# A hybrid decoder layer on one core: the sums of left operands and the late block sums of the second part move from GpSimd to VectorE

## The chip, the core and the metric

The kernel runs on one core of a Trainium2 chip. A core has five engines with instruction queues of their own: TensorE (PE in the profile, with its weight loads as PEld), VectorE (DVE), ScalarE (ACT), GpSimd (POOL) and SyncE (SP, which here only issues DMAs). Each queue is worked off in order; engines wait for each other through semaphores. The metric is the device time of one execution in microseconds, smaller is better.

## What is computed

One layer with two branches, on 2048 tokens and 16 meta tokens of width 1024, in float32:

```python
u = rmsnorm(hres, norm_w)
proj = jnp.einsum('bld,dn->bln', u, w_in)          # one projection for all
...                                                # branch 1: Mamba-2 SSD; branch 2: gated linear attention
branches = jnp.stack([y_ssd, y_gla], axis=2)
branch_proj = jnp.einsum('blnc,ncd->blnd', branches, w_branch)
gates = jax.nn.sigmoid(merge_g.reshape(b, l, N_BRANCH, D_MODEL))
merged = jnp.sum(gates * branch_proj, axis=2)
return hres + jnp.einsum('bld,de->ble', merged, w_out)   # then a final rmsnorm
```

The first part of the kernel computes the projections and the two branches; the second part computes the gates, the branch projections, the merge and the output projection, which are plain matrix products.

## The kernel before

**First part** (to about 1487 us). Four blocks of 512 tokens are projected and scanned. It isn't touched. Beside its work, GpSimd forms for later use the block sums of right operands of most stages (`make_sums` with a `store`; its line L84).

**Second part.** Seven stages follow each other: gate0, br00, br10 for the first half of the tokens, gate1, br01, br11 for the second half, and out. Each is a product of matrices that is done with seven instead of eight block products (the Strassen-Winograd scheme): a stage has 8 pairs (gate and out) or 4 (br), two pairs are worked on together, and each pair needs seven products p in the order 1, 2, 6, 7, 5, 3, 4. There are 280 products. A product is four accumulated steps of three matmuls each (L193 to L195): both operands are split into a high and a low half in float32r, and high-high, high-low and low-high are added up.

What a product needs:

- **Right operands** `br` (128 x 512, raw) are loaded by SP at L1011, 28 for each stage, through 5 buffers. ACT writes the high half of `b` (L1016), DVE subtracts it for the low half (L1017). When DVE has done so, the buffer of `br` is free and SP can load the next.
- **Left operands** `ar` are loaded by SP at L1023, four blocks a11, a12, a21, a22 for each pair, through 8 buffers, which is two pairs. From them come four sums: s1 = a21 + a22 (L1031), s2 = s1 - a11 (L1032), a21 = a11 - a21 in place (L1033) and s4 = a12 - s2 (L1034). GpSimd makes them. For each product ACT then writes the high half of `a` (L1040) and DVE the low half (L1041), five products ahead, into 7 buffers. An `ar` buffer is free when the last of these readers is done.
- **Results.** Products 1, 6 and 5 are copied from PSUM to `sn` by ACT (L1057). DVE adds `sn` to a PSUM bank (L1068: psc or psb); in the br stages it multiplies by the gate (L1094), in the out stage it adds the residual (L1117) and, after a norm (L1121 to L1132), GpSimd's queue stores the rows. PSUM bank `psa` can only take the next product when `sn` has been copied, and `psb` can only take product 4 when L1068 has read product 5.
- **Late block sums.** The right operands' sums of br01 and br11 can't be formed in the first part, since the tokens come last. `make_sums` is called for them with `store` None: SP loads four blocks (L80), GpSimd makes four differences of 128 x 256 (L84), and GpSimd's queue stores them two products later. There are 16 such units, eight in gate0 and eight in gate1, five products apart.

GpSimd's queue also issues all stores of the second part (L991, and L994 with an addition in memory).

The order on PE and on SP is written out: a table `todo` gives each load and preparation a place relative to the products (a right operand is loaded 3.2 places ahead of its preparation, a left one 7.5 ahead of its first product). On DVE, ACT and GpSimd a scheduler puts the instructions in order, by a timing of its own, when the kernel is built.

Of the kernel before, what the change touches and what calls it, by code (L numbers as in the profile page):

```python
# [12 lines left out]
ALU = mybir.AluOpType  # L13
# [27 lines left out]
def trunk_kernel(ctx: ExitStack, tc: tile.TileContext, xm, xmt, w_feat, w_tok, w_zm, w_br, w_o,  # L41
                 cf32, cmsk, pvec, fnw, hvec, gw2, out):
    nc = tc.nc
# [5 lines left out]
    def mk(pool, shape, dt, tag, **kw):  # L49
        cnt[0] += 1  # L50
        return pool.tile(shape, dt, tag=tag, name=f"{tag}_{cnt[0]}", **kw)
# [24 lines left out]
    def make_sums(pool, tag, nb, braw, sums, j, c, store):  # L76
        cs = slice(c * HB, (c + 1) * HB)
        pair = [mk(pool, [P, 512], F32, tag, bufs=nb).rearrange("p (i c) -> p i c", i=2) for _ in range(2)]
        for r, (k, t) in zip((t[:, i] for t in pair for i in range(2)), ((0, 1), (0, 0), (1, 1), (1, 0))):
            nc.sync.dma_start(r, braw(4 * k + j, t)[:, cs])  # L80
        yield
        (b12, b11), (b22, b21) = [(t[:, 0], t[:, 1]) for t in pair]
        for o, x, y in ((b11, b12, b11), (b12, b22, b12), (b22, b22, b11), (b21, b21, b22)):
            nc.gpsimd.tensor_tensor(o, x, y, op=ALU.subtract)  # L84
        if store is None:
            for dst, src in zip(sums, pair):
                late_store(dst[j][:, :, cs], src, 2)
            return
        yield
        yield  # L90
        for dst, src in zip(sums, pair):
            store.dma_start(dst[j][:, :, cs], src)
# [3 lines left out]
    def late_store(dst, src, lag=1):  # L96
        stores.setdefault(step_no[0] + lag, []).append((dst, src))
# [295 lines left out]
    def new_block(b, u):  # L393
        o = Block()
        o.b, o.u = b, u
        o.m0 = META if b == 0 else 0
        o.tt = o.m0 + BLK
        o.segs_all = [(0, o.tt // 2), (o.tt // 2, o.tt // 2)] if b == 0 else [(0, BLK)]
        o.segs_real = [(o.m0, BLK)]
        o.starts = [o.m0 + c * P for c in range(NCH)]  # L400
        o.chunks = ([(0, META)] if o.m0 else []) + [(a, P) for a in o.starts]
        o.ci0 = 1 if o.m0 else 0
        o.nck = len(o.chunks)
        for nm in ("tkd", "tkc", "ntc", "wde", "ecu", "dec"):
            setattr(o, nm, mk(bpool, [P, 5, NH], F32, nm, bufs=1))
        o.cumd = mk(dpool, [NH, BLK], F32, "cumd")
        o.g_all = mk(bpool, [P, GH, META + BLK], F32, "g_all")
        o.both = None
        if o.m0:
            o.both = mk(early, [P, KT, 2 * META], F32R, "both", bufs=1)  # L410
            for i in range(2):
                nc.gpsimd.tensor_copy(o.both[:, :, i * META:(i + 1) * META], u[i][:, :, :META].bitcast(F32))
        o.alr = mk(bpool, [P, 5, 48], F32, "alr")
        o.mov = lambda kt, a, n: tuple(t[:, kt, a:a + n] for t in u)
        return o
# [515 lines left out]
    def beside_unit(key):  # L931
        for j in range(4):
            for c in range(2):
                yield from make_sums(early, "wr", NWR, *sums[key], j, c, nc.sync)

    with tc.manual_schedule(engines={mybir.EngineType.PE, mybir.EngineType.SP}):
        for b in range(nblk):
            o = new_block(b, next_u[b])
# [45 lines left out]
    store = late_store  # L984
# [11 lines left out]
    class Stage:  # L996
# [23 lines left out]
        def load_a(self, n):  # L1020
            def raw(i, j):
                t = mk(rpl, [P, 4, P], F32, "ar")
                nc.sync.dma_start(t, self.araw(n, i, j))  # L1023
                return t

            if n not in self.a:
                self.a[n] = raw(0, 0), raw(0, 1), raw(1, 0)
                return
            (a11, a12, a21), a22 = self.a[n], raw(1, 1)
            s1, s2, s4 = [mk(spl2, [P, 4, P], F32, "as") for _ in range(3)]  # L1030
            nc.gpsimd.tensor_tensor(s1, a21, a22, op=ALU.add)  # L1031
            nc.gpsimd.tensor_tensor(s2, s1, a11, op=ALU.subtract)  # L1032
            nc.gpsimd.tensor_tensor(a21, a11, a21, op=ALU.subtract)  # L1033
            nc.gpsimd.tensor_tensor(s4, a12, s2, op=ALU.subtract)  # L1034
            self.a[n] = {1: a11, 2: a12, 3: s4, 4: a22, 5: s1, 6: s2, 7: a21}

        def prep_a(self, n, p):
# [140 lines left out]
    begun_at = [begins[3 * s] for s in range(nsb)]  # L1178
    spots = [g + 9 + 5 * k for g in begun_at for k in range(8)]
    late_sums = [make_sums(opl, "io", 8, *sums[key], j, c, None) for key in late for j in range(4) for c in range(2)]  # L1180
    for pos, gen in zip(spots, late_sums):
        for k in range(2):
# [104 lines left out]
```

## Time and profile before

| | |
|---|---|
| median of 3 runs | 2296.2 us (2296.17 to 2300.63) |
| profiled execution | span 2298.3 us from the first to the last instruction |
| second part: first product to last | 1487.4 to 2283 us |
| L1031 to L1034 on GpSimd | 160 of 128 x 512, means 1476 to 1653 ns |
| L84 on GpSimd in the second part | 64 of 128 x 256, means 867 and 913 ns |

The execution's own time is not listed apart from its span. In the rows of the profile, `a<-ar` says that tile `a` is written from tile `ar` (buffer numbers left out). A row of the timeline gives start, duration, engine, line and operation, and in brackets the idle time ahead of it with what ended it; x2 means that two instructions were put together. A row of groups gives busy time in us, mean in ns, then the engine's idle time ahead of it. A row of windows gives the stretch, its length, the busy time of PE, PEld, DVE, ACT and POOL with the number of instructions, the granted clock of TensorE, the busy share of the DMA engines and GB/s.

### The profile page before, as it was taken

The page shows a single profiled execution, that of the slowest core. Times are in us where ns is not written, and L with a number is a line of the kernel's source. Part 1 is how long each engine was busy: PE and PEld are TensorE (multiplying, and loading weights), DVE is VectorE, ACT ScalarE, POOL GpSimd, SP SyncE. Part 2 cuts the span into 40 slices and gives each one's busy share as a digit, 9 for nine tenths or more (in the row PEclk, how much of TensorE's full clock was granted, in tenths as well). Part 3 has the DMA queues.
Part 4 walks back from the last instruction along what each step waited for, and adds up shares of the span by engine and source line. Part 5 has one row for each costly group of instructions (what it writes and reads, how often), then busy time and mean ns, then how long its engine had stood idle before and what let it go on. Part 6 is the DMA issues. An engine that isn't in the chain of part 4 may idle for free.

```text
span 2298.3 us, 36496 instructions
## 1 busy us (share of the span) xinstructions
PE 2223.2 (97%) x12599; PEld 1938.7 (84%) x12599; DVE 1646.5 (72%) x3108; ACT 1119.4 (49%) x2508; POOL 789.6 (34%) x869
## 2 busy tenths in 40 slices
PE   6899999999999999999999999989999999999998
PEld 6899888888889889888988898868787788788786
DVE  5787767687765687775678656687778855788775
ACT  5565554463444454444445434554644545454443
POOL 3344533122221122212212100158535476535452
PEclk9999999999999999999999999999999999999999
DMA  7767866667886676886677654466767866679653
GB/s 254 232 221 245 296 211 208 211 193 246 267 264 208 205 225 208 272 278 206 203 215 230 215 184 149 149 221 205 264 233 223 249 216 213 233 251 252 182 185 110
DMA packets 281866, 507.51 MB, mean 221 GB/s; under 512 B 27104, under 2 KB 134880, under 8 KB 281680
## 3 DMA queue, kind: packets, MB, share of 16 engines
q1 hardware_dynamic: 217232, 413.76, 55.7%
q0 software_dynamic: 17568, 50.87, 7.3%
q10 hardware_dynamic: 46880, 40.54, 5.4%
q8 instruction: 99, 1.62, 0.3%
q14 instruction: 87, 0.71, 0.1%
HBM read 357.87 MB, written 147.19 MB: 220 GB/s over the span
## 4 chain that ended last, share of the span: by engine, by line
PE 73%; DVE 9%; DMA 9%; issue 4%; ACT 3%; POOL 2%; SPq 1%; ACTq 0%; POOLq 0%; DVEq 0%
PE pj L193 13%; PE pj L195 13%; PE pj L194 13%; PE psa L193 4%; PE psa L195 4%; PE psa L194 4%; DMA br<-br_t 2%; PE psb L195 2%; PE psb L193 2%; PE psb L194 2%; DVE b L1017 2%; PE pc L619 2%; PE pc L789 2%; PE pc L889 1%; PE pc L620 1%
## 5 line engine op out<-in xcount | busy, mean ns | idle before, releaser
L193 PE MATMUL pj<-u,whl 128*128 128x512 f32 (+1 forms) x1184 | 445.5, 376 | 9.4 <-ACT acc L529 4.5
L195 PE MATMUL pj<-u,whl 128*128 128x512 f32 (+1 forms) x1184 | 429.5, 363 | 0.0
L194 PE MATMUL pj<-u,whl 128*128 128x512 f32 (+1 forms) x1184 | 428.9, 362 | 0.0
L193 PE MATMUL pj<-whl,u 128*128 128x256 f32 (+1 forms) x992 | 288.8, 291 | 2.8 <-ACT u L261 2.2
L195 PE MATMUL pj<-whl,u 128*128 128x256 f32 (+1 forms) x992 | 282.4, 285 | 0.2 <-DVE u L266 0.2
L194 PE MATMUL pj<-whl,u 128*128 128x256 f32 (+1 forms) x992 | 282.1, 284 | 0.0
L193 PE MATMUL psa<-b,a 128*128 128x512 f32 x640 | 252.3, 394 | 18.1 <-ACT sn L1057 17.9
L193 PEld LDWEIGHTS pj<-u,whl 128*128 128x128 f32 x1184 | 223.6, 189 | 47.2 <-ACT acc L529 5.4
L195 PEld LDWEIGHTS pj<-u,whl 128*128 128x128 f32 x1184 | 223.2, 188 | 35.6
L194 PEld LDWEIGHTS pj<-u,whl 128*128 128x128 f32 x1184 | 223.9, 189 | 33.1
L194 PE MATMUL psa<-b,a 128*128 128x512 f32 x640 | 250.2, 391 | 0.9 <-DVE b L1017 0.9
L195 PE MATMUL psa<-b,a 128*128 128x512 f32 x640 | 250.5, 391 | 0.0
L84 POOL TENSOR_TENSOR wr<-wr 128x256 f32<-128x256 f32 x80 | 64.2, 803 | 428.8 <-DMA wr<-u 163.4
L181 POOL TENSOR_TENSOR whl<-wr,whl 128x512 fp32r<-128x512 f32 (+1 forms) x100 | 138.3, 1389 | 187.2 <-ACT whl L180 154.8
L1041 DVE TENSOR_TENSOR a<-ar,a 128x512 fp32r<-128x512 f32 x160 | 157.3, 993 | 61.9 <-ACT a L1040 61.4
L1017 DVE TENSOR_TENSOR b<-br,b 128x512 fp32r<-128x512 f32 x196 | 159.1, 833 | 49.1 <-ACT b L1016 48.8
L193 PEld LDWEIGHTS pj<-whl,u 128*128 128x128 f32 x992 | 189.8, 191 | 4.5 <-ACT u L261 2.3
L195 PEld LDWEIGHTS pj<-whl,u 128*128 128x128 f32 x992 | 189.8, 191 | 0.8 <-DVE u L266 0.8
L194 PEld LDWEIGHTS pj<-whl,u 128*128 128x128 f32 x992 | 189.9, 191 | 0.4
L1016 ACT ACTIVATE b<-br 128x512 fp32r<-128x512 f32 x196 | 120.1, 628 | 125.2 <-DMA br<-br_t 53.6
L533 DVE SCALAR_TENSOR_TENSOR acc<-cin,hcw,acc 128x512 f32<-128x512 f32 (+1 forms) x192 | 161.3, 840 | 11.4 <-ACT acc L529 9.3
L193 PEld LDWEIGHTS psa<-b,a 128*128 128x128 f32 x640 | 120.9, 189 | 49.3 <-ACT sn L1057 24.7
(297 smaller groups left out, 5064.5 us busy)
## 6 DMA issues: line engine op xcount, KB each, us to landing
whl<-k_s SPq DMA_DIRECT2D x96, 512.0 KB, 4.4
whl<-k_g SPq DMA_DIRECT2D x96, 512.0 KB, 4.2
whl<-k_v SPq DMA_DIRECT2D x48, 512.0 KB, 4.0
whl<-k_z SPq DMA_DIRECT2D x36, 512.0 KB, 4.1
wr<-in_w_feat SPq DMA_DIRECT2D x64, 256.0 KB, 4.4
k_s<-whl SPq DMA_DIRECT2D x32, 512.0 KB, 3.8
cb<-cumd ACTq DMA_DIRECT2D x64, 256.0 KB, 5.8
k_g<-whl SPq DMA_DIRECT2D x32, 512.0 KB, 3.8
```

The source lines that it names most:

```text
L84: nc.gpsimd.tensor_tensor(o, x, y, op=ALU.subtract)
L181: nc.gpsimd.tensor_tensor(hl[:, 1], raw, hl[:, 0].bitcast(F32), op=ALU.subtract)
L193: nc.tensor.matmul(ps, sh, mh, start=first, stop=False, **kw)
L194: nc.tensor.matmul(ps, sh, ml, start=False, stop=False, **kw)
L195: nc.tensor.matmul(ps, sl, mh, start=False, stop=last, **kw)
L533: nc.vector.scalar_tensor_tensor(acc, cin[:, k:k + tt], hcw[:, ti, k:k + 1], acc, op0=ALU.mult, op1=ALU.add)
L619: nc.tensor.matmul(py[:, h * 64:(h + 1) * 64], dm[:, h], xdt[:, h], start=True, stop=True)
L620: nc.tensor.matmul(py[:, 256:512], cf[:, a:a + P], s_ssd[:, g], start=True, stop=True)
L789: nc.tensor.matmul(ps[:, r * P:(r + 1) * P], kq[:, 2 * r * P:(2 * r + 1) * P], kq[:, (2 * r + 1) * P:(2 * r + 2) * P], start=True, stop=True)
L1016: nc.scalar.activation(t[:, 0], raw, AF.Copy)
L1017: nc.vector.tensor_tensor(t[:, 1], raw, t[:, 0].bitcast(F32), op=ALU.subtract)
L1041: nc.vector.tensor_tensor(t[:, 1], src, t[:, 0].bitcast(F32), op=ALU.subtract)
```

## The change

The four sums of left operands are issued on VectorE, in all seven stages, and so are the differences of `make_sums` where `store` is None, which is the late ones. The block sums beside the first part stay on GpSimd, as do all stores.

```diff
-            nc.gpsimd.tensor_tensor(o, x, y, op=ALU.subtract)
+            (nc.vector if store is None else nc.gpsimd).tensor_tensor(o, x, y, op=ALU.subtract)
...
-            nc.gpsimd.tensor_tensor(s1, a21, a22, op=ALU.add)
-            nc.gpsimd.tensor_tensor(s2, s1, a11, op=ALU.subtract)
-            nc.gpsimd.tensor_tensor(a21, a11, a21, op=ALU.subtract)
-            nc.gpsimd.tensor_tensor(s4, a12, s2, op=ALU.subtract)
+            nc.vector.tensor_tensor(s1, a21, a22, op=ALU.add)
+            nc.vector.tensor_tensor(s2, s1, a11, op=ALU.subtract)
+            nc.vector.tensor_tensor(a21, a11, a21, op=ALU.subtract)
+            nc.vector.tensor_tensor(s4, a12, s2, op=ALU.subtract)
```

224 instructions leave GpSimd's queue and join DVE's. The orders of PE and SP stay the same, word for word; on DVE and ACT the scheduler rearranges the second part. Three places follow; a row with + stands there now, one with - stood there before, and the others stand in both.

DVE at the start of the second part, from rstd (the last norm of the first part) to the second `b2`; `b2` are the right operands of product 2, `end_g` belongs to the first part's end:

```order
 L241 TENSOR_SCALAR rstd_2956_17162<-ssq_2944_17087 128x4
+L1031 TENSOR_TENSOR as_2965_17303<-ar_2963_17299,ar_2964_17301 128x512
+L1032 TENSOR_TENSOR as_2966_17304<-as_2965_17303,ar_2961_17295 128x512
+L1033 TENSOR_TENSOR ar_2963_17299<-ar_2961_17295,ar_2963_17299 128x512
 L1041 TENSOR_TENSOR a_2984_17348<-ar_2968_17310,a_2984_17348 128x512
+L1034 TENSOR_TENSOR as_2967_17305<-ar_2962_17297,as_2966_17304 128x512
 L1041 TENSOR_TENSOR a_2989_17363<-ar_2962_17297,a_2989_17363 128x512
+L1031 TENSOR_TENSOR as_2972_17318<-ar_2970_17314,ar_2971_17316 128x512
 L1041 TENSOR_TENSOR a_2994_17374<-ar_2969_17312,a_2994_17374 128x512
+L1032 TENSOR_TENSOR as_2973_17319<-as_2972_17318,ar_2968_17310 128x512
+L1033 TENSOR_TENSOR ar_2970_17314<-ar_2968_17310,ar_2970_17314 128x512
 L1041 TENSOR_TENSOR a_2999_17389<-as_2966_17304,a_2999_17389 128x512
```

Right behind these rows comes the first `b2` (L1017), then `end_g`, the eighth sum, `end_g` again and the second `b2`; ahead of the third and of the fourth `b2` there are now two L1041 each, which stood behind them before.

DVE at the handover from gate1 to br01; `b6` and `b7` are right operands of br01, the first two `a` are the last ones of gate1 (product 4), `as` are sums for br01:

```order
 L1017 TENSOR_TENSOR b6_3778_21518<-br_3750_21413,b6_3778_21518 128x512
+L1041 TENSOR_TENSOR a_3758_21442<-ar_3696_21106,a_3758_21442 128x512
 L1017 TENSOR_TENSOR b6_3781_21538<-br_3756_21427,b6_3781_21538 128x512
-L1041 TENSOR_TENSOR a_3758_21442<-ar_3696_21106,a_3758_21442 128x512
 L1017 TENSOR_TENSOR b6_3784_21546<-br_3760_21448,b6_3784_21546 128x512
+L1031 TENSOR_TENSOR as_3763_21468<-ar_3754_21422,ar_3762_21466 128x512
 L1041 TENSOR_TENSOR a_3766_21475<-ar_3705_21145,a_3766_21475 128x512
+L1032 TENSOR_TENSOR as_3764_21469<-as_3763_21468,ar_3752_21418 128x512
+L1033 TENSOR_TENSOR ar_3754_21422<-ar_3752_21418,ar_3754_21422 128x512
 L1017 TENSOR_TENSOR b7_3788_21569<-br_3768_21481,b7_3788_21569 128x512
```

and ACT at the same place, where `sn` is the copy of a product:

```order
 L1016 ACTIVATE b6_3778_21518<-br_3750_21413 128x512
-L1016 ACTIVATE b6_3781_21538<-br_3756_21427 128x512
 L1057 ACTIVATE sn_3744_21385<-psa_3724_21266 128x512
 L1040 ACTIVATE a_3758_21442<-ar_3696_21106 128x512
+L1016 ACTIVATE b6_3781_21538<-br_3756_21427 128x512
 L1016 ACTIVATE b6_3784_21546<-br_3760_21448 128x512
```

On both engines the first `a` moved ahead of `b6_3781`, and one sum now stands ahead of the second `a`.

DVE at the handover from br11 to out, with the right operands `b6` and `b7` of out, the last `a` of br11 (a_4070) and sums of out:

```order
 L1017 TENSOR_TENSOR b6_4089_23010<-br_4063_22908,b6_4089_23010 128x512
+L1031 TENSOR_TENSOR as_4066_22928<-ar_4056_22880,ar_4065_22926 128x512
 L1041 TENSOR_TENSOR a_4070_22937<-ar_4006_22615,a_4070_22937 128x512
+L1032 TENSOR_TENSOR as_4067_22929<-as_4066_22928,ar_4054_22876 128x512
+L1033 TENSOR_TENSOR ar_4056_22880<-ar_4054_22876,ar_4056_22880 128x512
+L1034 TENSOR_TENSOR as_4068_22930<-ar_4055_22878,as_4067_22929 128x512
 L1041 TENSOR_TENSOR a_4082_22978<-ar_4054_22876,a_4082_22978 128x512
 L1017 TENSOR_TENSOR b7_4092_23032<-br_4072_22943,b7_4092_23032 128x512
```

One sum came ahead of a_4070, and three ahead of the next `a` and `b7`.

## The prediction

> **What bounds the kernel now.** I read the page first, for the busiest engine.
>
> ```profile
> PE 2223.2 (97%) x12599; PEld 1938.7 (84%) x12599; DVE 1646.5 (72%) x3108; ACT 1119.4 (49%) x2508; POOL 789.6 (34%) x869
> ```
>
> PE is the bound of the whole. The change touches only the second part, so I cut that part into windows and read busy time by engine (the first number behind the stretch is its length).
>
> ```profile
> 1493.00:1513.00 20.00, 12.33 (x51) 9.29 (x49) 18.42 (x21) 11.96 (x24) 10.24 (x10) 0.83 0.41 138
> ...
> 1640.00:1650.00 10.00, 7.75 (x33) 5.77 (x32) 8.02 (x8) 5.58 (x10) 9.92 (x7) 1.00 0.74 250
> 1650.00:1720.00 70.00, 70.00 (x310) 57.98 (x310) 51.00 (x71) 36.40 (x65) 22.93 (x27) 1.00 0.68 237
> ...
> 1798.00:1830.00 32.00, 28.82 (x117) 22.69 (x117) 29.91 (x37) 16.82 (x31) 17.91 (x14) 0.95 0.82 225
> ...
> 1956.00:1966.00 10.00, 4.31 (x15) 3.19 (x14) 7.63 (x7) 3.53 (x6) 8.14 (x6) 0.86 0.68 219
> ...
> 2120.00:2157.00 37.00, 32.56 (x142) 25.97 (x141) 28.77 (x39) 18.11 (x35) 15.33 (x13) 1.00 0.89 235
> ...
> sum 789.00, PE 763.20 PEld 625.76 DVE 590.63 ACT 387.88 POOL 411.50; mean PE 63.60 PEld 52.15 DVE 49.22 ACT 32.32 POOL 34.29
> ```
>
> The sum row covers 1493 to 2282: PE idles 789.0 - 763.2 = 25.8 us. That idle time, and a few us of half clock behind it (the granted clock of 0.83 and 0.86), is all that any change here can win. It lies in knots: 7.7 us at the start (1493), then 2.3, 3.2, 5.7 and 4.4 us where one stage hands over to the next. Between them PE is full (1650:1720: 70/310 = 0.226 us a matmul, so a product of 12 matmuls takes 2.7 us). DVE at 591 of 789 (75%) is next. The table of waits says whom PE waits for.
>
> ```profile
> PE psa L193 <- ACT sn L1057: 17.9, 13, 5.7
> PE psc L194 <- DVE b L1017: 6.7, 2, 4.0
> ```
>
> **What DVE pays for GpSimd's sums.** The groups of instructions, with their means in ns:
>
> ```profile
> L1041 DVE TENSOR_TENSOR a<-ar,a 128x512 fp32r<-128x512 f32 x159 | 156.6, 995 | 61.9 <-ACT a L1040 61.4
> L1017 DVE TENSOR_TENSOR b<-br,b 128x512 fp32r<-128x512 f32 x192 | 156.5, 836 | 48.6 <-ACT b L1016 48.4
> L1041 DVE TENSOR_TENSOR a<-as,a 128x512 fp32r<-128x512 f32 x120 | 125.7, 1048 | 37.7 <-ACT a L1040 36.8
> L1068 DVE TENSOR_TENSOR sn<-sn,psb 128x512 f32<-128x512 f32 x78 | 53.1, 682 | 35.3 <-ACT sn L1057 24.6 <-PE psb L195 10.5
> ...
> L84 POOL TENSOR_TENSOR io<-io 128x256 f32<-128x256 f32 x32 | 28.7, 913 | 0.1
> ...
> L779 DVE TENSOR_TENSOR sq<-sq,act 128x256 f32<-128x256 f32 x14 | 5.9, 422 | 1.0 <-ACT sq L778 0.5 <-PE pt L871 0.2
> ```
>
> L1068 has the same shape, runs in the same stretches, and takes 682 ns; it reads one operand from PSUM. L1041 and L1017 read both from SBUF and average 836 to 1048. The surplus is 159 x 0.313 + 120 x 0.366 + 192 x 0.154 = 123 us. That it comes from GpSimd's sums is seen at single rows of the start:
>
> ```profile
> 1497.64 5.07 DVE L1017 TENSOR_TENSOR b<-br,b 128x512 fp32r<-128x512 f32 x1
> ...
> 1498.44 1.28 POOL L1032 TENSOR_TENSOR as<-as,ar 128x512 f32<-128x512 f32 x1
> ...
> 1500.88 1.27 POOL L1034 TENSOR_TENSOR as<-ar,as 128x512 f32<-128x512 f32 x1
> ...
> 1502.77 0.79 PE L194 MATMUL psc<-b,a 128*128 128x512 f32 x1 [4.03 <-DVE b L1017]
> ...
> 1512.64 2.49 DVE L1017 TENSOR_TENSOR b<-br,b 128x512 fp32r<-128x512 f32 x4
> ```
>
> One L1017 stood 5.07 us while GpSimd ran its sums from 1498.44 to 1502.15, and PE waited 4.03 us for it. With GpSimd silent, four took 2.49 us: (2.49 - 0.69)/3 = 0.60 us apart.
>
> **The load of DVE.** Added: 160 sums L1031 to L1034 at 0.68 us (the L1068 row) = 109 us, and 64 of L84 at 0.42 us (the L779 row) = 27 us, together 136 us. Removed: the 123 us. DVE's load hardly moves, whereas GpSimd gives up nearly all its arithmetic here. The removal is the unknown: at none of it DVE would stand at 727 of 789 us (92%), at all of it near 604. I take all, because of the 682 of L1068. So the time is decided by order, not by load; I follow it through the knots.
>
> **Start: -3 us.** As the order shows, DVE does eleven other operations between rstd (row below) and the first L1017, which itself is the twelfth.
>
> ```profile
> 1489.65 0.17 DVE L241 TENSOR_SCALAR rstd<-ssq 128x4 f32<-128x4 f32 x1 [1.05 <-ACT junk L896]
> ```
>
> 1489.8 + 12 x 0.60 + about 0.4 for sums that wait for the one ahead = 1497.4, as before (1497.7). The second L1017 is four places on, at 1499.9 instead of 1502.7; the third and fourth come behind two L1041 each, at 1501.7 and 1503.5. PE then waits in three short pieces, and ends this product about 2 us earlier. The two L1017 for the next products follow at once and not several us later, which takes 1 us more.
>
> **gate1 to br01, the 5.7 us gap: -3.4 us.** The chain in rows:
>
> ```profile
> 1951.22 0.63 ACT L1016 ACTIVATE b<-br 128x512 fp32r<-128x512 f32 x1 [3.69 <-DMA br<-br_t]
> ...
> 1952.90 1.40 DVE L1041 TENSOR_TENSOR a<-ar,a 128x512 fp32r<-128x512 f32 x1 [0.31 <-ACT a L1040]
> ...
> 1955.91 1.78 DVE L1041 TENSOR_TENSOR a<-ar,a 128x512 fp32r<-128x512 f32 x1
> ...
> 1954.32 3.73 SPq L1023 DMA_DIRECT2D ar<-in_w_br  x2
> 1958.10 0.43 SPq L1011 DMA_DIRECT2D br<-br_t  x1
> ...
> 1961.67 1.30 ACT L1016 ACTIVATE b<-br 128x512 fp32r<-128x512 f32 x2 [6.73 <-DMA br<-br_t]
> ...
> 1963.51 0.80 PE L193 MATMUL psa<-b,a 128*128 128x512 f32 x1 [5.69 <-ACT sn L1057]
> ```
>
> SP stood at two loads of left operands until the two L1041 freed their slots (ends 1954.30 and 1957.69); only then, at 1958.10, came the right operands for which ACT waited ahead of the copy sn that PE needed. After the change ACT and DVE do the first of these L1041 ahead of the b that waits until 1951.2, so it no longer holds SP. The second follows two L1017 and one sum: ACT's b ends at 1951.85, then four steps of 0.60, so it ends near 1954.3, 3.4 us earlier. SP, the loads, ACT and PE move with it.
>
> **Other boundaries: about -0.6 us in sum.** Here the change also hurts:
>
> ```profile
> 2114.47 2.40 DVE L1041 TENSOR_TENSOR a<-ar,a 128x512 fp32r<-128x512 f32 x2
> ...
> 2115.04 1.28 POOL L1031 TENSOR_TENSOR as<-ar,ar 128x512 f32<-128x512 f32 x1 [6.80 <-DMA ar<-m]
> ...
> 2115.18 0.52 SPq L1023 DMA_DIRECT2D ar<-m  x1
> ...
> 2122.43 0.50 PE L193 MATMUL psa<-b,a 128*128 128x512 f32 x1 [1.45 <-ACT sn L1057]
> ...
> 2143.17 0.50 PE L193 MATMUL psa<-b,a 128*128 128x512 f32 x1 [1.41 <-ACT sn L1057]
> ```
>
> The sum, whose operand landed at 2115.0, now stands ahead of the L1041 that releases SP at 2115.18; that L1041 ends near 2116.3, +1.1 us on this gap. The like holds, at 0.6 us each, at three more boundaries (gate0 to br00, br00 to br10, br01 to br11): +2.9. Behind it, each operation that ran beside a sum at 1.7 us now takes 0.60, so the later loads of the same handover leave 1 to 3 us earlier; I count -1 on the gap of 1.41 at 2143, and as much on the later gaps of two more handovers (around 1744 and 1827) = -3, and -0.5 at 1805, where the releasing L1041 was itself slowed. The 64 operations of L84 lie in the gate stages, where PE hardly idles; their loads landed before DVE reaches most of them, so they cost nothing. If that cover were gone, 27 us.
>
> **Sum:** -3 - 3.4 + 2.9 - 3 - 0.5 = **-7 us**. It is made in an execution of 2298.3 us of span (its own time apart from the span isn't listed); the median of the runs is 2296.2, 2.1 below, and what lies around these knots is unchanged, so: 2289.
>
> **A rule weighed.**
>
> ```profile
> 1805.66 0.50 PE L193 MATMUL psa<-b,a 128*128 128x512 f32 x1 [2.54 <-ACT sn L1057]
> ...
> 1806.71 0.63 PE L193 MATMUL psa<-b,a 128*128 128x512 f32 x1
> ...
> 2155.94 0.50 PE L193 MATMUL psa<-b,a 128*128 128x512 f32 x1 [1.58 <-ACT sn L1057]
> ```
>
> Behind 2.54 us of idle time the matmuls lasted 0.63 us, behind 1.58 they didn't slow down. The gap that I shorten to 5.7 - 3.4 = 2.3 us lies between the two, so the sum leaves its slow matmuls (about 8 at 0.2 us more) in. The Trainium skill, "TensorE: Matmul & The Clock Gate", section "Part 1: The HAM clock gate", has the clock halved after an idle window of about 3.4 us; the 2.54 us here disagree, and by that rule the sum would be -8.6.
>
> **Rivals.** (1) *Full clock behind the shortened gap*: -7 - 1.6, **2287**. For it: 1.58 us did no harm. Against: 2.54 did. (2) *The loads pace the handovers, and the gains and delays cancel*: the 5 slots of br and loads of several us stay. If start and gate1 to br01 bring half (-3.2) and the second gaps gain only 1: -3.2 + 2.9 - 1 = -1.3, **2295**. For it: ACT's waits in these rows end with DMAs. (3) *Slower: DVE, in order, now waits where GpSimd waited alone.*
>
> ```profile
> 2223.18 0.69 DVE L1117 SCALAR_TENSOR_TENSOR io<-sn,io 128x512 f32<-128x512 f32 x1
> ...
> 2228.56 1.43 POOL L1031 TENSOR_TENSOR as<-ar,ar 128x512 f32<-128x512 f32 x1 [6.73 <-DMA ar<-m]
> ```
>
> In the new order this sum stands ahead of the L1117 of 2223.18, so DVE stops for some 5.4 us, and behind it L1041s and the L1068 that frees psb. PE needs that bank three products (8 us) after it was filled; DVE catches up at 0.60 us a step with about 3 us to spare, and L1041s are made five products (13 us) ahead. Should the operand land over 3 us later than here, each us more stops PE. At eight such places 1.5 us each: -7 + 12 = +5, **2301**. Against: the spare time. (4) *The change does nothing*, were DVE's surplus not GpSimd's; 2296, counted with (2): the 5.07 row speaks against it.
>
> **How the numbers follow.** Forecast 0.55 (own range 2283 to 2292), (1) 0.08, (2) and (4) 0.22, (3) 0.15. A measurement of this kernel can tell about 0.2%, 4.6 us. Forecast's upper end, 0.05, lies within that, so faster 0.58, same 0.27, slower 0.15. The range runs from 2280 (a little more than twice the forecast gain, still within the idle time) to 2301, which leaves out half of (3) and the case where none of DVE's surplus goes.
>
> **What would show it.** Right: L1041 and L1017 at a mean near 690 ns, DVE near 600 us, the start's idle time at 4 to 5 us, the 5.7 us gap near 2.3, the one at 2122 longer. Wrong: L1041 staying near 1000 ns; new PE gaps within stages, at psb, with DVE idle ahead of L1031; SP waiting longer for L1041.

## The result, and the profile after

| | before | after |
|---|---|---|
| median of the runs | 2296.8 us (6 runs, 2292.74 to 2300.63) | 2285.4 us (6 runs, 2279.01 to 2290.58) |
| ratio after / before | | 0.9941 (95% interval 0.9925 to 0.9958) |
| profiled span | 2298.3 us | 2288.8 us |
| second part, first product to last | 799.4 us | 784.2 us |

The change makes the kernel 11 us faster by the medians and 13.5 by the ratio. Forecast were 7, so the direction and the range held and the gain was larger than worked out. The last row is the sharper measure, and by it the gain is 15 us, twice the forecast: in the profiles below, the second part begins anywhere from 1483.0 to 1493.1 us although the first part's work is the same in all but the last of them, and this scatter of 10 us lies in every single time. The rows of windows over the second part, of the kernel before and then of the change (stretch, length, busy PE, PEld, DVE, ACT, POOL, clock, DMA):

```profile
1487.45:2286.80 799.35, 773.55 (x3371) 633.60 (x3370) 598.11 (x746) 394.28 (x727) 416.29 (x426) 0.99 0.69 218
...
1493.08:2277.28 784.20, 771.69 (x3371) 633.46 (x3370) 577.67 (x970) 394.35 (x727) 130.68 (x203) 0.99 0.70 222
```

TensorE's idle time falls from 799.35 - 773.55 = 25.8 us to 12.5. VectorE does 224 instructions more and is busy 20 us *less*. The groups of the change say why:

```profile
L1017 DVE TENSOR_TENSOR b<-br,b 128x512 fp32r<-128x512 f32 x192 | 127.8, 688 | 30.6 <-ACT b L1016 30.2
L1041 DVE TENSOR_TENSOR a<-ar,a 128x512 fp32r<-128x512 f32 x160 | 109.5, 689 | 70.1 <-ACT a L1040 69.8
L1041 DVE TENSOR_TENSOR a<-as,a 128x512 fp32r<-128x512 f32 x120 | 82.7, 690 | 28.1 <-ACT a L1040 27.3
L1068 DVE TENSOR_TENSOR sn<-sn,psb 128x512 f32<-128x512 f32 x80 | 54.8, 685 | 22.1 <-PE psb L195 12.7 <-ACT sn L1057 9.1
L1031 DVE TENSOR_TENSOR as<-ar,ar 128x512 f32<-128x512 f32 x40 | 27.6, 690 | 29.4 <-DMA ar<-m 19.7 <-DMA ar<-in_w_feat 6.4 <-DMA ar<-in_w_br 3.1
...
L84 DVE TENSOR_TENSOR io<-io,io 128x256 f32<-128x256 f32 x32 | 13.5, 423 | 0.4
```

L1041, 995 and 1048 ns before, and L1017, 836 before, all take what L1068 always took. VectorE now waits 29 us ahead of L1031 for loads that GpSimd used to wait for. TensorE's waits in the second part of the change:

```profile
PE psa L193 <- ACT sn L1057: 8.6, 7, 2.2
PE psc L194 <- DVE b L1017: 3.2, 4, 1.6
```

They were 17.9 and 6.7 us.

To see where the time went I add up, for every matmul of the second part, the time from one start to the next beyond the usual 0.2265 us (so slow matmuls at half clock count too), by place. "again" is a second profile of the same program, taken as e5 below.

| us lost at | before | change | change again | forecast for the change |
|---|---|---|---|---|
| start | 11.8 | 9.8 | 9.3 | -3 |
| gate0 to br00 | 2.8 | 4.0 | 2.3 | +0.6 |
| br00 to br10 | 1.7 | 0 | 0 | +0.6 - 1 |
| br10 to gate1 | 5.6 | 2.6 | 1.7 | -1 - 0.5 |
| gate1 to br01 | 7.5 | 2.4 | 3.9 | -3.4 |
| br01 to br11 | 0.5 | 0 | 2.0 | +0.6 |
| br11 to out | 5.2 | 1.3 | 1.5 | +1.1 - 1 |
| sum | 35.2 | 20.2 | 20.7 | -7 |

The count takes in the first part's last matmuls, which lie among the first products. The sums of two profiles of one program agree within 0.5 us, the single places only within 2. For e5 each place's idle time was expected within 1 us of the first profile's, and the median at 2282 to 2288; br01 to br11 missed it, with 1.76 us of idle time instead of none.

### The profile page after: what moved, and what is told of

It reads as the page before. It is cut to its first block, busy times and chain, and to the rows that moved or that the text cites. A ratio compares the mean times of both kernels' runs of the same rounds, so it can differ in the third digit from the quotient of the medians.

```text
span 2288.8 us, 36364 instructions
## 1 busy us (share of the span) xinstructions
PE 2224.8 (97%) x12599; PEld 1941.6 (85%) x12599; DVE 1624.2 (71%) x3332; ACT 1119.7 (49%) x2508; POOL 507.4 (22%) x645
## 4 chain that ended last, share of the span: by engine, by line
PE 78%; DVE 7%; DMA 6%; issue 3%; ACT 3%; POOL 1%; SPq 1%; ACTq 0%; POOLq 0%; DVEq 0%
PE pj L193 13%; PE pj L195 13%; PE pj L194 13%; PE psa L193 5%; PE psa L195 5%; PE psa L194 5%; PE psb L195 3%; PE psb L194 3%; PE psb L193 3%; PE pc L619 2%; PE pc L789 2%; PE psc L195 1%; PE psc L194 1%; PE psc L193 1%; PE pc L620 1%
## 5 line engine op out<-in xcount | busy, mean ns | idle before, releaser
L1016 ACT ACTIVATE b<-br 128x512 fp32r<-128x512 f32 x196 | 119.7, 627 | 86.7 <-DMA br<-br_t 36.7
L84 POOL TENSOR_TENSOR wr<-wr 128x256 f32<-128x256 f32 x80 | 67.2, 840 | 424.3 <-DMA wr<-u 174.0
L1041 DVE TENSOR_TENSOR a<-ar,a 128x512 fp32r<-128x512 f32 x160 | 109.5, 689 | 70.1 <-ACT a L1040 69.8
L1017 DVE TENSOR_TENSOR b<-br,b 128x512 fp32r<-128x512 f32 x196 | 130.5, 688 | 31.3 <-ACT b L1016 30.9
```

Source lines behind the costliest of these rows:

```text
L84: (nc.vector if store is None else nc.gpsimd).tensor_tensor(o, x, y, op=ALU.subtract)
L1016: nc.scalar.activation(t[:, 0], raw, AF.Copy)
L1017: nc.vector.tensor_tensor(t[:, 1], raw, t[:, 0].bitcast(F32), op=ALU.subtract)
L1041: nc.vector.tensor_tensor(t[:, 1], src, t[:, 0].bitcast(F32), op=ALU.subtract)
```

## Experiments

The theory: GpSimd's sums stretched VectorE's operations on two SBUF operands, and the chains of such steps at the handovers and at the start became longer; without it they are short, and VectorE has the time for the sums. Rivals: the scheduler's new order on VectorE and ScalarE brought the gain (R1); GpSimd's queue is free for the stores sooner (R2); VectorE's load decides, whatever it is made of (R3). Each run stands against the kernel before, whose median was 2296.7 to 2299.1 us in these comparisons.

| | median us | ratio to before (95%) | second part us |
|---|---|---|---|
| e1 left sums only | 2290.1 | 0.9969 (0.9959 to 0.9979) | 789.4 |
| e2 late sums only | 2302.8 | 1.0028 (1.0017 to 1.0038) | 801.1 |
| e3 change + GpSimd additions | 2374.3 | 1.0332 (1.0312 to 1.0352) | 867.1 |
| e4 change + GpSimd memsets | 2286.7 | 0.9957 (0.9941 to 0.9973) | 788.3 |
| e5 change again | 2281.9 | 0.9929 (0.9914 to 0.9944) | 784.6 |
| e6 change, 10 left buffers | 2274.9 | 0.9895 (0.9881 to 0.9910) | 776.2 |
| e7 before, 10 left buffers | 2304.5 | 1.0023 (1.0012 to 1.0034) | 799.7 |
| e8 no sums at the start | 2281.8 | 0.9919 (0.9904 to 0.9934) | 780.6 |
| e9 first pairs only | 2287.7 | 0.9957 (0.9943 to 0.9971) | 789.2 |
| e10 more work on VectorE | 2285.0 | 0.9943 (0.9923 to 0.9964) | 786.1 |
| e11 9 left, 6 right buffers | 2283.9 | 0.9942 (0.9920 to 0.9965) | 781.1 |
| e12 all block sums | 2288.3 | 0.9964 (0.9949 to 0.9978) | 777.2 |

### e3 and e4: is it the stretching?

To the change, behind the sums in `load_a`, for e3 and for e4 (`dead` is a tile of its own, set to zero at the start):

```diff
+            [nc.gpsimd.tensor_tensor(dead, dead, x, op=ALU.add) for x in (a22, dead, dead, dead)]
```

```diff
+            nc.gpsimd.tensor_tensor(dead[:, 0, 0:1], dead[:, 0, 0:1], a22[:, 0, 0:1], op=ALU.add)
+            [nc.gpsimd.memset(dead, 0.0) for _ in range(10)]
```

e3:

> The change, and behind each set of left sums GpSimd does four additions of 128x512 on a tile that nobody uses, the first with a22 as operand, so that they start when the sums started before. It leaves the result as it is; orders of TensorE, SyncE are those of the change, VectorE's and ScalarE's nearly so. Theory (stretching): L1041 and L1017 go back to means of 900 to 1050 ns, VectorE carries the stretch and the sums, some 700 us of the 790, and the time goes back to the one before or past it: 2295 to 2310. Rival 1 (order): within 3 us of the change, 2282 to 2289, though VectorE's means rise. Rival 2 (GpSimd's queue): 2295 or more, and the next kernel as well.

e4:

> The change, and behind each set of left sums GpSimd does a wait on a22 of one column and ten memsets of 128x512 on a tile that nobody uses: its queue is as busy as before, but it reads no SBUF operands. Theory (stretching by operands read from SBUF): L1041 and L1017 stay under 750 ns and the time within 3 us of the change, 2282 to 2289. Rival 1 (order): the same. Rival 2 (GpSimd's queue holds up stores): 2293 or more with VectorE's means near 690 ns. If memsets stretch VectorE too, its means show it, and the time follows them.

Groups of e3 (the second part):

```profile
L1035 POOL TENSOR_TENSOR dead<-dead 128x512 f32<-128x512 f32 x120 | 161.7, 1348 | 8.0
L1041 DVE TENSOR_TENSOR a<-ar,a 128x512 fp32r<-128x512 f32 x160 | 132.8, 840 | 46.4 <-ACT a L1040 46.2
...
L1033 DVE TENSOR_TENSOR ar<-ar,ar 128x512 f32<-128x512 f32 x40 | 55.4, 1385 | 0.0
```

Groups of e4:

```profile
L1035 POOL MEMSET dead<- 128x512 f32 x400 | 215.8, 539 | 20.7
L1041 DVE TENSOR_TENSOR a<-ar,a 128x512 fp32r<-128x512 f32 x160 | 109.3, 688 | 67.9 <-ACT a L1040 67.4
...
L1033 DVE TENSOR_TENSOR ar<-ar,ar 128x512 f32<-128x512 f32 x40 | 27.4, 685 | 0.0
```

160 additions on GpSimd, of which nobody uses the result, cost 92 us against the change (2374.3 against 2281.9; 83 us by the second parts), far more than expected; the stretch falls mostly on the sums, which run beside them (L1033 from 686 to 1385 ns), less on L1041 (840 instead of the 900 to 1050 expected). 400 memsets, which keep GpSimd about as busy, stretch nothing and cost 1 to 5 us. So R2 falls (e4), and R1 falls as the whole cause: e3 has nearly the change's order (on VectorE 962 of the second part's 983 instructions stand in the same succession) and none of its gain. That the order brings a part of the gain isn't excluded by e3; e10 bears on it. GpSimd slows VectorE by reading SBUF, not by being busy. The Trainium skill, "SBUF — State Buffer", section "Who interferes with whom", says just this: a VectorE instruction with two SBUF inputs contends with a GpSimd instruction that reads SBUF, not with one that only writes it. The 688 and the 1385 ns agree.

### e10: is it VectorE's load?

The same four additions on VectorE instead:

```diff
+            [nc.vector.tensor_tensor(dead, dead, x, op=ALU.add) for x in (a22, dead, dead, dead)]
```

> The change, and behind each set of left sums VectorE does four more additions of 128x512 on a tile that nobody uses: 160 instructions, about 97 us at 0.60, without GpSimd. VectorE then has some 680 us to do in 785, as in the kernel before, but nothing is stretched. The scheduler sets its order anew. Theory: within the stages this costs nothing; where the additions stand in the chain of a handover each costs 0.6, so up to 2.4 us at the start and at each of six handovers: 3 to 12 us over the change. If load without stretching costs nothing at all: within 2 us of the change. If load is what made the kernel before slow: back to it, 10 us or more over the change.

The second part of e10, and three rows of its timeline (VectorE, then TensorE):

```profile
1488.64:2274.71 786.07, 769.96 (x3371) 631.60 (x3370) 662.76 (x1131) 393.03 (x727) 129.14 (x203) 1.00 0.70 222
...
2226.85 0.69 DVE L1031 TENSOR_TENSOR as<-ar,ar 128x512 f32<-128x512 f32 x1 [1.22 <-DMA ar<-m]
...
2229.87 0.68 DVE L1068 TENSOR_TENSOR sn<-sn,psb 128x512 f32<-128x512 f32 x1
...
2230.60 0.50 PE L193 MATMUL psb<-b,a 128*128 128x512 f32 x1 [2.84 <-DVE sn L1068]
```

VectorE is busy 663 us of 786, 65 more than in the kernel before, and the time is that of the change within 2 us of second part. R3 falls: load as such is nearly free, a stretched chain is not. The rows show one price: at two places in the out stage a sum, and the additions with it, hold the L1068 behind them until TensorE lacks `psb`. That is the slower rival of the prediction; it needed twice the work to appear, and gaps of 1.43 and 2.84 us came of it.

The near equality is a balance, though. Counted as in the table, e10 loses about 6.8 us at the start (the change 9.8 and 9.3) and 6.7 from br11 to out on (the change 1.3 and 1.5). Its order at the start is another: the second L1017 begins 1.2 us behind the first, and not 2.5 as in the change. So an order can be worth some 3 us at one place, and the additions cost more than the sum shows. On VectorE e10's order is far from the change's (700 of 983 instructions in the same succession) and the gain is about the same, so the gain doesn't hang on the change's own order; what part of it the new order brings at single places stays open.

### e1 and e2: the two halves

e1 is the change with L84 as before, e2 the kernel before with this line of the change:

```diff
-            nc.gpsimd.tensor_tensor(o, x, y, op=ALU.subtract)
+            (nc.vector if store is None else nc.gpsimd).tensor_tensor(o, x, y, op=ALU.subtract)
```

e1:

> Half of the change: the left operands' sums (L1031 to L1034) on VectorE, the late block sums (L84) still on GpSimd. Theory: the gain comes from VectorE's operations no longer being stretched by GpSimd's sums of two SBUF operands, and the left sums are nearly all of those that run beside handovers, so nearly all of the 11.4 us should be there: 8 to 11 us under the kernel before. L1041 and L1017 at means of 700 to 740 ns (stretched only beside the 64 L84). Rival 1 (the scheduler's new order on VectorE and ScalarE brings the gain): also near the full gain, since the order is mostly that of the change. Rival 2 (GpSimd's queue is free for the stores sooner): near the full gain too, as 160 of 224 operations leave it.

e2:

> The other half: the late block sums (L84) on VectorE, the left operands' sums still on GpSimd. Theory: the L84 lie in the two gate stages, where TensorE hardly idles, so 0 to 2 us under the kernel before; L1041 near 950 to 1000 ns as before, since the left sums stretch it still. If the late sums were the larger part, 5 us or more under.

The halves don't add up: 7 us gained and 6 lost alone, 13 to 16 gained together by the ratios. By the second parts e1 gains 10.0 us, e2 loses 1.7, and the change gains 15. e1 comes near the 8 to 11 us expected of it; e2, expected at 0 to 2 us under, went the other way. For e2 the timeline shows where (VectorE, GpSimd, TensorE):

```profile
1842.36 0.91 DVE L84 TENSOR_TENSOR io<-io 128x256 f32<-128x256 f32 x1 [2.79 <-DMA io<-y]
1843.06 1.35 POOL L1032 TENSOR_TENSOR as<-as,ar 128x512 f32<-128x512 f32 x1
1843.31 2.83 DVE L84 TENSOR_TENSOR io<-io,io 128x256 f32<-128x256 f32 x2
...
1846.17 1.92 DVE L84 TENSOR_TENSOR io<-io 128x256 f32<-128x256 f32 x1
...
1848.01 0.68 DVE L1068 TENSOR_TENSOR sn<-sn,psb 128x512 f32<-128x512 f32 x1
...
1849.89 0.61 PE L193 MATMUL psa<-b,a 128*128 128x512 f32 x1 [4.10 <-ACT sn L1057]
```

VectorE stood 2.79 us for the load of a late sum, then took 5.7 us for four sums that take 1.7 in the change, since GpSimd's left sums ran beside them. L1068 came behind, then ScalarE's copy, then TensorE, 4.1 us late. So a sum on VectorE that waits does harm where the sums left on GpSimd stretch it as well. For e1, L1041 at 748 ns shows the remaining stretch, little over what was expected, but the 5 us that its second part is longer than the change's lie at the start (+1), br00 to br10 (+1.6) and gate1 to br01 (+2.4), not beside L84. As the change again differs by 2 us at such places, what e1 lacks isn't settled.

### e9: which sums matter

```diff
-            nc.vector.tensor_tensor(s1, a21, a22, op=ALU.add)
+            (nc.vector if n < 2 else nc.gpsimd).tensor_tensor(s1, a21, a22, op=ALU.add)
...
```

and so for all four.

> The change, but the left sums on VectorE only for the first two pairs of each stage (14 of 40 sets, those that are made around the handovers); the other 26 sets are back on GpSimd. Theory (the stretching costs at the handovers, within the stages VectorE has slack): 60 to 100% of the gain stays, 2282 to 2290 beside a change of 2282 to 2286, with L1041 at a mean between the two, 850 to 950 ns. Rival (VectorE's load as such decides): the gain goes with the share of sums, a third of it stays, 2290 to 2296.

10 of the change's 15 us are there with 14 of 40 sets, at a mean of 877 ns for L1041 of `ar`. The start and gate1 to br01 lose 9.1 and 2.1 us, as in the change. Of what is missing, one gap of 3.95 us at 1841 is e2's accident over again (VectorE 3.43 us idle ahead of L84, then four sums beside GpSimd's). So most of the gain comes from the left sums at the start and the handovers, together with the late ones, which are on VectorE here too.

### e6, e7, e11: SyncE at the handovers

```diff
-    rpl = pool2("rawa", 8)
+    rpl = pool2("rawa", 10)
```

on the change (e6) and on the kernel before (e7); e11 has 9 there, and 6 instead of 5 in `rawb`.

e6:

> The change with 10 instead of 8 buffers for left operands. My reading of the handovers (SyncE stands at loads of left operands until the releasing L1041, and the right operands behind them come late for ScalarE's copy): SyncE no longer stands there, the right operands leave 3 to 4 us earlier, and the gaps left at gate0 to br00 and gate1 to br01 (2.2 us of idle time each) go to 0 to 0.5; 3 to 6 us under the change. Rival: the 5 buffers of right operands hold SyncE at the same places; within 1.5 us of the change, and the gaps stay over 1.5 us.

e7:

> The kernel before with 10 instead of 8 buffers for left operands, sums on GpSimd as before. By the same reading the 5.7 us gap at gate1 to br01 goes to 0 to 1.5 us although VectorE stays stretched (L1041 near 1 us); 4 to 8 us under the kernel before. The start stays at 10 to 12 us lost. If stretching alone made the gaps, with the loads early or late: within 2 us of the kernel before.

e11:

> The change with 9 buffers for left and 6 for right operands (the same room as 10 and 5). If both hold SyncE at the handovers: like 10 and 5 or 2 us better. If only the left ones do: half of what 10 and 5 gave, 3 to 4 us under the change instead of 7, as one of the two loads that SyncE stands at still waits.

e6 is 7 us faster than the change on the same chip (2274.9 against 2281.9), and **beats both kernels**. Its second part, and TensorE's waits in it:

```profile
1485.42:2261.66 776.24, 769.35 (x3371) 632.76 (x3370) 577.47 (x970) 396.05 (x727) 128.07 (x203) 1.00 0.70 225
...
PE psc L194 <- DVE b L1017: 3.7, 4, 1.6
PE psa L193 <- ACT sn L1057: 2.4, 4, 0.9
```

All that was left between stages is gone but 2.4 us, and 10.0 of the 12.4 us still lost lie at the start. That confirms the reading for the *change*. For the kernel before it fails: e7 isn't faster but slower by 0.2%. In e7 at gate1 to br01 (VectorE, SyncE, GpSimd, TensorE):

```profile
1957.14 5.98 SPq L1011 DMA_DIRECT2D br<-br_t  x3
1957.24 1.60 POOL L1031 TENSOR_TENSOR as<-ar,ar 128x512 f32<-128x512 f32 x1 [8.31 <-DMA ar<-in_w_br]
1957.59 1.79 DVE L1017 TENSOR_TENSOR b<-br,b 128x512 fp32r<-128x512 f32 x1
1958.91 1.62 POOL L1032 TENSOR_TENSOR as<-as,ar 128x512 f32<-128x512 f32 x1
1959.31 1.78 DVE L1041 TENSOR_TENSOR a<-ar,a 128x512 fp32r<-128x512 f32 x1
1960.50 1.72 POOL L1033 TENSOR_TENSOR ar<-ar,ar 128x512 f32<-128x512 f32 x1
1961.01 1.76 DVE L1017 TENSOR_TENSOR b<-br,b 128x512 fp32r<-128x512 f32 x1
...
1970.14 0.80 PE L193 MATMUL psa<-b,a 128*128 128x512 f32 x1 [4.17 <-ACT sn L1057]
```

SyncE no longer stands at left operands; it stands at right ones, whose buffers wait for L1017, and VectorE makes one step each 1.7 us, in turn with GpSimd. The left operands that came earlier only let the two engines overlap more (L1041 of `ar` at 1203 ns in e7). The buffers are worth 7 us once the stretching is gone, and nothing before. e11 has the change's ratio, though its second part is 3 us shorter. The first of its two forecasts, 7 us or more under the change, holds by neither measure; the second, 3 to 4 us, holds by the second part alone.

### e8: the start

```diff
+            if self is stages[0] and n < 2:
+                self.a[n] = {1: a11, 2: a12, 3: a12, 4: a22, 5: a21, 6: a22, 7: a21}
+                return
```

> The change without the left sums of gate0's first two pairs: products 3, 5, 6, 7 of these read raw blocks in the sums' place, so eight of VectorE's operations at the start are left out. My step says the start is a chain of VectorE steps 0.60 us apart: the first two waits for L1017 fall by the six sums ahead of them, 3 to 4 us less lost at the start (now 9.8, then 6 to 7) and elsewhere nothing; 2 to 4 us under the change. Rival: the start waits for something else (the loads of right operands, ScalarE): under 1 us.

The kernel leaves out sums that the layer needs, so only its time is of use. A miss at the start, which lost 8.6 us instead of 9.3 to 9.8 where 6 to 7 were expected, and the median is the change's. The second part is 3.8 us shorter than the change's, but most of that lies at places that scatter by 2 us. Without the sums ScalarE is the next to be late; rows of e8 (TensorE):

```profile
1491.89 0.49 PE L193 MATMUL psc<-b,a 128*128 128x512 f32 x1 [1.48 <-ACT b L1016]
...
1493.88 0.57 PE L194 MATMUL psc<-b,a 128*128 128x512 f32 x1 [1.49 <-DVE b L1017]
```

Its L1016 stands behind the left operands' high halves (L1040, in this kernel L1043) in its queue. So leaving the sums out is worth about 1 us at the start, not the 4.8 of eight steps.

### e12: does it carry to the first part?

On e6, `make_sums` uses VectorE always: 160 L84 beside the first part move too, in two forms of 80 (the expectation counted one).

```diff
-            (nc.vector if store is None else nc.gpsimd).tensor_tensor(o, x, y, op=ALU.subtract)
+            nc.vector.tensor_tensor(o, x, y, op=ALU.subtract)
```

> The change with ten left buffers, and the block sums beside the first part (80 of L84, 840 ns each on GpSimd, at 0.42 on VectorE some 34 us) on VectorE as well. If the move carries over: GpSimd's L84 no longer stretch VectorE's steps of the first part, whose idle time on TensorE is 1487 - 1449 = 38 us; 2 to 8 us under the change with ten buffers. Rival: in the first part L181 (100 of 1384 ns) stays on GpSimd and stretches VectorE anyway, and VectorE in its queue now waits for the loads of these sums, which GpSimd waited for alone (174 us of its idle time stand ahead of L84): no gain, or some us lost, with VectorE idle ahead of L84.

It doesn't: 13 us slower than e6 by the medians (on another chip; 16 by the ratios), and by the profiles it is the first part: the second begins at 1497.5 (1483.0 to 1493.1 elsewhere) and is as short as in e6. VectorE's group in e12, the first part:

```profile
L84 DVE TENSOR_TENSOR wr<-wr 128x256 f32<-128x256 f32 x80 | 34.5, 432 | 44.1 <-DMA wr<-u 18.6 <-DMA wr<-y 15.6 <-DMA wr<-in_w_o 5.9
```

In its queue VectorE waits 44 us for their loads, as the rival of the expectation said, and that there would be no gain was right. The rival's other reason holds at most in part: the stretching did shrink (the 256 operations of L607 take 302 ns in the mean instead of 357 in e6). TensorE idles 28.6 us of the first part from 22 us on, 20.5 in e6, and the added waits end with ScalarE (L650, 5.8 us instead of 0.9) and VectorE (L892, 5.0 instead of 1.7). That the waits for loads made them isn't shown: the longest, 1.79 us at 1236, has no such wait in the 10 us ahead of it, and the new order is a rival that no run tells apart.

## Why the prediction was right, and where its sizes were off

The mechanism was right, but the sum, -7, is less than half of the 15 us that the second part gained. One term made most of the difference, the other boundaries. That the medians come nearer to the forecast (11 us) is luck, most likely the scatter of the first part: in e5 the same program is 17 us under the kernel before.

- **What bounds, and VectorE's load: right.** All the surplus went (means of 682 to 690 ns) and VectorE is busy 578 us of 784, near the 604 of 789 forecast; e3 and e4 show that it was GpSimd's reads.
- **gate1 to br01: right by its rows.** In the change (SyncE, VectorE, ScalarE, TensorE):

```profile
1951.22 1.29 DVE L1017 TENSOR_TENSOR b<-br,b 128x512 fp32r<-128x512 f32 x2 [2.34 <-ACT b L1016]
...
1952.43 0.68 DVE L1031 TENSOR_TENSOR as<-ar,ar 128x512 f32<-128x512 f32 x1
...
1953.03 0.69 DVE L1041 TENSOR_TENSOR a<-ar,a 128x512 fp32r<-128x512 f32 x1
...
1953.75 0.33 SPq L1023 DMA_DIRECT2D ar<-in_w_br  x1
1954.13 2.32 SPq L1011 DMA_DIRECT2D br<-br_t  x5
...
1958.87 0.63 ACT L1016 ACTIVATE b<-br 128x512 fp32r<-128x512 f32 x1 [0.44 <-DMA br<-br_t]
...
1959.41 0.58 ACT L1057 ACTIVATE sn<-psa 128x512 f32<-128x512 f32 x1
...
1960.04 0.50 PE L193 MATMUL psa<-b,a 128*128 128x512 f32 x1 [2.16 <-ACT sn L1057]
```

Two L1017, one sum, the releasing L1041, 0.60 us apart, then SyncE, the loads, ScalarE's copy: a gap of 2.16 us, 2.3 forecast. The place gave 5.1 and 3.6 us, 3.4 forecast; what is over in the first profile is the clock (below). e6 shows that these loads were its cause: the place loses nothing there.
- **Start: the steps right, the term too large.** The idle pieces at the start are 0.7, 1.1, 1.6, 0.3 and 0.2, together 3.9 us where 4 to 5 were forecast and 7.7 stood before; the second L1017 began 2.52 us behind the first, 2.5 forecast. But only 2.0 to 2.5 us came of it, not 3: the windows have a granted clock of 0.83, as before, and 0.91 in the second profile (20 us from 5.5 us behind the first product, change and change again):

```profile
1498.60:1518.60 20.00, 16.82 (x62) 12.22 (x61) 18.83 (x32) 14.92 (x29) 2.39 (x4) 0.83 0.58 188
...
1491.45:1511.45 20.00, 16.25 (x66) 12.06 (x65) 19.13 (x32) 15.22 (x29) 2.39 (x4) 0.91 0.57 189
```

Several short waits kept the clock low for as long as two long ones in the first profile, and for nearly as long in the second.
- **Other boundaries, -0.6: the step that failed.** They gave about -8: gate0 to br00, br00 to br10, br10 to gate1 and br01 to br11 together lost 10.6 us before and 6.6 and 6.0 in the two profiles of the change, br11 to out 5.2 before and 1.3 and 1.5 after. Two mistakes are seen at br11 to out, where the gap at 2122 was to become longer and became shorter. The delay of +1.1 was right where it was worked out: counted from the end of the product ahead of the gap (2120.98 before, 2115.45 after), SyncE issued the right operands at 2112.03 instead of 2116.41, that is 1.15 us later. But the load wasn't later. SyncE's issue and ScalarE's wait for it, before and after:

```profile
2116.41 0.90 SPq L1011 DMA_DIRECT2D br<-out_t  x2
...
2121.26 0.63 ACT L1016 ACTIVATE b<-br 128x512 fp32r<-128x512 f32 x1 [3.28 <-DMA br<-out_t]
...
2112.03 0.90 SPq L1011 DMA_DIRECT2D br<-out_t  x2
...
2115.26 0.63 ACT L1016 ACTIVATE b<-br 128x512 fp32r<-128x512 f32 x1 [3.25 <-DMA br<-out_t]
...
2116.43 0.50 PE L193 MATMUL psa<-b,a 128*128 128x512 f32 x1 [0.98 <-ACT sn L1057]
```

On the same count ScalarE starts 0.5 us *earlier* (2115.26 - 2115.45 against 2121.26 - 2120.98), since the load took 2115.2 - 2112.0 = 3.2 us instead of 4.8. Why the load was shorter no run shows; it took 3.5 us in the second profile. I passed a delay of the issue on one for one. And the gaps further on (1.41 and 1.58 us before, at 2143 and 2156) were gone whole, and those at 1744 and 1827 too, where I had counted three times 1 us.

The next largest miss is br10 to gate1, 3.0 and 3.9 us gained where 1.5 were forecast. The gap of 2.54 us at 1805 became 0.74 (1.41 in the second profile), without slow matmuls behind it. SyncE's issue there, before and after:

```profile
1800.88 0.90 SPq L1011 DMA_DIRECT2D br<-gate_t  x2
...
1801.64 0.90 SPq L1011 DMA_DIRECT2D br<-gate_t  x2
```

Counted from the end of the product ahead of the gap (1803.12 and 1805.60), the issue came 1.7 us earlier, and not 0.5. The 0.5 was right for the releasing L1041, one step and one sum instead of a slowed step; but the right operand ahead of it had already landed 1.2 us earlier by the same count. I worked each gap out from load times taken from the kernel before, and the chain ahead of them had become shorter too.
- **Late sums at no cost: nearly so in the change, not alone.** In the change VectorE waits 0.6 us in all for their loads. Behind a wait of 2.37 us for a left sum's load and 0.62 for a late one's, at 1840 to 1841, a new gap of 1.33 us stands at 1846 in one of its two profiles. Alone they aren't free (e2, 6 us lost by the ratio, 1.7 by the second part).
- **The clock behind the gap**: the slow matmuls forecast at gate1 to br01 stayed away in the first profile of the change and stood there in the second; behind an equal gap at gate0 to br00 it was the other way round (see the end).
- **The slower rival** was the right mechanism with the wrong weight: VectorE does stop ahead of L1031 (29 us) and L84, but its slack covers nearly all of it. e2, e9 and e10 show the gaps that come where it doesn't.

## What to carry to other kernels

Look for VectorE operations on two SBUF operands that take longer than the same shape with one operand in PSUM: where GpSimd reads SBUF beside them, moving its work *onto* VectorE can make VectorE less busy, and shorter steps in a chain are worth more than the load that comes with them. Move all of the work that reads SBUF in that stretch, as a part of it alone can lose (e2), and measure each stretch by itself: the same move lost time in the first part (e12). A fix that does nothing (more buffers, e7) may be worth trying again once another limit is gone (e6).

## What the runs showed of the hardware

While both engines have two-operand work, VectorE and GpSimd take turns at about 1.7 us a step for each (e7's rows), where VectorE alone steps each 0.60 us.

The clock behind a gap isn't decided by the gap's length alone. Two gaps of the change (TensorE):

```profile
1648.63 0.52 PE L193 MATMUL psa<-b,a 128*128 128x512 f32 x1 [2.17 <-ACT sn L1057]
1648.97 0.61 PE L194 MATMUL psa<-b,a 128*128 128x512 f32 x1
...
1960.38 0.40 PE L194 MATMUL psa<-b,a 128*128 128x512 f32 x1
```

Behind 2.17 us the matmuls take 0.61, behind 2.16 (the row at 1960.04 above) 0.40. In twelve profiles of the second part (all but e3 and e12, past the start) none of the gaps under 1.87 us was followed by slow matmuls, 9 of the 19 from 1.87 to 2.84 were, and all five from 3.6 us on. The prediction's bound, between 1.58 and 2.54, was a band and not a line. The Trainium skill, "TensorE: Matmul & The Clock Gate", section "Part 1: The HAM clock gate (the "warmup" mystery)", lets the clock fall after an idle window of about 3.4 us, and has that window run freely. By the length alone gaps of 1.9 to 2.8 us shouldn't suffice, and 9 of 19 did; here the measurement decides. That the place of a gap in the window decides between equal gaps would fit, but no run here shows it.
